# One more whole tile before the Winograd chains, fillers moved between cycles, token sums spread

## The chip, the cores and the metric

The kernel runs on one core of a Trainium2 chip. The metric is the device time of one execution in microseconds. The engines named here are PE (matrix multiply), DVE (vector engine), ACT (scalar engine), POOL (which here only issues transfers) and SP (which issues transfers too). Each works through its own instructions strictly in the order in which they were emitted, and waits where an operand, or a buffer that it writes, is not ready.

## The reference

A decoder trunk of two layers on one sequence of 512 tokens of width 1024, float32. Layer 0 mixes tokens by attention over three groups of heads with different dilations, layer 1 by a gated linear recurrence. After each mixer stands a gated feed-forward block, and each of these four parts is wrapped in RMS norms with a residual:

```python
def conv_ffn(x, w_up, conv_w, conv_b, w_down):
    u = causal_dwconv(x @ w_up, conv_w, conv_b)          # width 6144, 3 taps along the tokens
    g, v = u[..., :D_FF], u[..., D_FF:]
    return (jax.nn.gelu(g, approximate=True) * v) @ w_down

# per layer: x = x + rms_norm(mixer(rms_norm(x)));  x = x + rms_norm(conv_ffn(rms_norm(x)))
```

The change concerns the two feed-forward blocks: their up projection (1024 to 2 times 3072 features) and its beginning.

## The kernel before, in words

**Arithmetic.** Every float32 operand of a product is split into two rounded halves, high and low: ACT copies the operand into the high half (`split`, L211), DVE subtracts it from the operand to get the low half (L212). A product then takes three matmuls: high times high, high times low, low times high.

**The up projection.** The 3072 hidden features are worked through in 12 groups `j` of 256, each with a gate half and a value half of 256 columns. A 128-column piece of it for all 512 tokens is called a tile; `b` 0 and 1 are the two gate tiles of a group, 2 and 3 its two value tiles. After the matmuls of a tile, `begin` (L880 on) starts the convolution: ACT writes the own tap and bias into `u` (L859), DVE adds the two other taps (L863, two instructions of 128x511 and 128x510), and then ACT applies gelu to a gate tile (L881), or DVE multiplies a value tile into its gate tile (L885).

Groups 0 and 1 are computed directly; a tile is 48 matmuls of 256 columns. Groups 2 to 11 (`SEVEN`) are computed with a Winograd form of Strassen's scheme: a 256-column half of a group is one "chain", which needs seven products of half the tokens by half the features instead of eight. There are 20 chains in a block. A chain's products are its steps, numbered 1, 5, 2, 6, 3, 7, 4 in their order of time; each is 12 matmuls of 256 columns. Steps 5, 6, 7, 4 multiply sums and differences of token blocks (`T`, called token sums), which `token_sums` makes on DVE (L1025, L1022) and splits once per block from copies `B` of the normed input. Steps of one chain share two PSUM banks: ACT copies the result of steps 1, 5 and 6 out to `part` (L1159) before a later step adds to the same place; DVE adds these back (L1163 after step 3, L1168 after step 7).

**Weights of a chain.** A `raw` buffer receives the four blocks of a chain's weights (SP, L408). Four sums of blocks are made in place, three by accumulating transfers that POOL issues (L248; `ahead`, `left`, `across`, each sent off once the split of the old value is done), one by DVE (L274). Seven splits give the seven left operands; they are written `w11`, `s1`, `w12`, `s2`, `s3`, `s4`, `a22`. At most 14 halves are alive at a time, and three raw buffers.

**Order of the work around the change.** In `seven` (L1177) all steps stand in numbered places: chain n has the cycle of ten places from 10n, with its steps at the places of `AT` (1: 0, 5: 1, 2: 2, 6: 4, 3: 5, 7: 8, 4: 13, so that step 4 falls into the next cycle). `free_slots` (L253) names the places in between that take fillers. The fillers are, first, the quarters of the two value tiles of group 1 (12 matmuls each, four to a tile, L1127 to L1129), and then the first products of the down projection (`rows`, two to each of 20 hidden tiles k), each of which needs a split of a row of down weights and a split of a finished hidden tile. A filler and a step take PE equally long. `slot` emits one place's matmuls, then what had been put off to it, then a tick. At each tick `pump` emits the next one or two splits, in an order that `stream` sets by due places, and steps that run beside (norms, token sums) go on by one after as many ticks as they last yielded.

**Before the chains**, the norm's last token tiles are transposed on PE and split (`transposed`, L570): ACT high half from PSUM, DVE low half from PSUM, and ACT's plain copy `B` from PSUM for the token sums (L588). Then come the gate and value tiles of group 0, in halves of the tokens; the two gate tiles of group 1, whole; and the chains.

Of the kernel before, what the change touches and what calls it, by code (L numbers as in the profile page):

```python
# [11 lines left out]
F32 = mybir.dt.float32  # L12
F32R = mybir.dt.float32r
I32 = mybir.dt.int32
AF = mybir.ActivationFunctionType
ALU = mybir.AluOpType
# [22 lines left out]
SEVEN = range(2, 12)  # L39
TAIL, REST = 16, range(20, 24)  # L40
AT = {1: 0, 5: 1, 2: 2, 6: 4, 3: 5, 7: 8, 4: 13}
CYCLE = 10
# [83 lines left out]
def kernel(  # L126
# [25 lines left out]
    nc = tc.nc  # L152
# [100 lines left out]
    def free_slots(n):  # L253

        end = CYCLE * n
        free = [CYCLE * c + r for c in range(n) for r in ((6, 7, 9) if c < 2 or c > 13 else (6, 7))][2:] + [end, end + 1]
        assert not {CYCLE * c + a for c in range(n) for a in AT.values()} & set(free)
        return free

    def stream(i0, n):  # L260

        items = []
        for c in range(n):
            i, o = i0 + c, CYCLE * c

            def left(i=i):
                add_block(i, "w11", 2)

            def across(i=i):
                add_block(i, "s1", 0)  # L270

            def lower(i=i):
                x = blocks(i)
                nc.vector.tensor_tensor(x["w12"], x["w12"], x["s1"], op=ALU.add)  # L274

            if c:
                items.append((o - 11, (None, lambda i=i: ahead(i))))
            for at, item in (
                (-6, ("w11", "w11")), (-5.9, (None, left)), (-4.4, ("s1", "s1")), (-4.3, (None, across)),
                (0.4, ("w12", "w12")), (5, ("s2", "s1")), (5.1, (None, lower)), (7, ("s3", "w11")),  # L280
                (8.5, ("s4", "w12")), (10.6, ("a22", "a22")),
            ):
                if isinstance(item[0], str):
                    item = ((i, item[0]), lambda i=i, h=item[1]: [blocks(i)[h]], item[0] == "a22")
                items.append((o + at, item))
        free = free_slots(n)
        direct = up["direct"]
        at = 8
        for key, loads, cuts, length in direct:
            u = free[at]  # L290
            if loads:
                items.append((u - EARLY, (None, loads)))
            items.append((u - 1, ((i0, key), cuts, False)))
            at += length
        return [item for _, item in sorted(items, key=lambda x: x[0])]
# [117 lines left out]
    def chunk():  # L413
        i = state["next"]
        state["next"] += 1
        return i
# [16 lines left out]
    def later(n, f):  # L433
        due.append([n, f])
# [109 lines left out]
    copies = {}  # L544
# [25 lines left out]
                nc.scalar.activation(o.rearrange("p (k b j) -> p k b j", k=4, j=32), src, AF.Copy)  # L570

    def transposed(t, xs, hT, keep):
        banks = []
        for i in range(2):
            ps = psum("tr")
            for k in range(4):
                nc.tensor.transpose(ps[:, k * P : (k + 1) * P], xs[i][:, k * P : (k + 1) * P], ident)
            ps3 = ps.rearrange("p (k c) -> p k c", k=4)
            hi = hT[0][:, 4 * i : 4 * i + 4, t * P : (t + 1) * P]
            lo = hT[1][:, 4 * i : 4 * i + 4, t * P : (t + 1) * P]  # L580
            nc.scalar.activation(hi, ps3, AF.Copy)
            nc.vector.tensor_tensor(lo, ps3, hi.bitcast(F32), op=ALU.subtract)
            banks.append(ps)
        if keep:
            copies[t] = []
            for ps in banks:
                o = gen(s="B")
                nc.scalar.activation(o, ps, AF.Copy)  # L588
                copies[t].append(o)

    def first_transposed(t, i, ks=range(4)):

# [112 lines left out]
    def feat_tile(i, m, hT, sink):  # L705
        ps = psum()
        W = take(i, m)
        for n in (0, 256):
            feat(W, hT, ps, n, n + 256)
        done()  # L710
        rest = sink(ps)
        tick()
        if rest:
            rest()
# [135 lines left out]
    def ffn(layer, hT, post, pre):  # L850
# [20 lines left out]
        def begin(b, ps, j, minus=False, apart=False):  # L871
            m = b % 2
            k = 2 * j + m
            u, taps = conv(ps, 24 * (b // 2) + k, minus)
            if apart:
                later(0, taps)
            else:
                taps()
            if b < 2:
                gv[k] = u  # L880
                return lambda: nc.scalar.activation(u, u, AF.Gelu_apprx_tanh)  # L881
            g = gv[k]

            def gate():
                nc.vector.tensor_tensor(g, g, u, op=ALU.mult)  # L885
                ready.add(k)

            return gate

        def tiles(j, i, bs):  # L890
            for b in bs:
                feat_tile(i, b % 2, hT, lambda ps: begin(b, ps, j))

        def gen_load(*srcs):
            o = []
# [13 lines left out]
        for k in range(REST[0]):  # L909
            w = ffn_w_down[layer][k * P : (k + 1) * P, 0:512].rearrange("(k p) c -> p k c", p=P)  # L910
            o, load = gen_load(w)
# [3 lines left out]
        T = []  # L915
        side(token_sums(T), 3)
        for j in range(SEVEN[0] - 1):
# [3 lines left out]
            else:  # L921
                feat_tiles(2, hT, lambda b, ps: begin(b, ps, j)(), True)
        tiles(SEVEN[0] - 1, chunk(), (0, 1))
        prep, run = down(act, post, pre)
        return run(seven(hT, T, begin, chunk(), lambda: prep(2)))

    def down(act, post, pre):

# [139 lines left out]
    def token_sums(T):  # L1068

        assert len(sides) == 1, len(sides)  # L1070
        d = dp.tile([P, 4, D], F32, name=nm("x_kept"))
        nc.gpsimd.dma_start(d, X[0])
        kept.append(d)
        wide = token_homes(False)
        T.extend([[h[:, 2 * k : 2 * k + 2] for k in range(2)] for h in wide[n : n + 2]] for n in range(0, 8, 2))
        b11, b12, b21, b22 = ([copies[t + a][i] for a in range(2)] for i, t in ((0, 0), (0, 2), (1, 0), (1, 2)))

        def part(n, a, b):
            hi, lo = (h[:, :, P * a : P * a + P] for h in wide[2 * n : 2 * n + 2])
            split(hi, lo, b[a].rearrange("p (k t) -> p k t", k=4))  # L1080

        for a in range(2):
            difference(b11[a], b11[a], b12[a])
        yield 1
        for a in range(2):
            part(0, a, b11)
        yield 1
        for a in range(2):
            difference(b12[a], b22[a], b12[a])
            negative(b22[a], b11[a], b22[a])  # L1090
        yield 1
        for a in range(2):
            part(1, a, b22)
        yield 1
        for a in range(2):
            part(2, a, b12)
        yield 1
        for a in range(2):
            negative(b21[a], b22[a], b21[a])
        yield 1  # L1100
        for a in range(2):
            part(3, a, b21)
# [71 lines left out]
    def seven(hT, T, begin, last, prep):  # L1174
# [4 lines left out]
        def finish(b, ps, j, minus=False):  # L1179
            later(2, begin(b, ps, j, minus, True))  # L1180
# [13 lines left out]
            if pair[-1] == 3:  # L1194
                done(2)

        fill = []
        for m in range(2):
            fill += quarters(last, m, hT, lambda ps, m=m: finish(2 + m, ps, SEVEN[0] - 1))
        fill += [lambda k=k, p=p: rows(k, p) for k in range(REST[0]) for p in ((0, 1), (2, 3))]  # L1200
        steps = {}
        n = 0
# [5 lines left out]
        free = free_slots(n)  # L1208
# [631 lines left out]
```

## Time and profile before

| what | us |
|---|---|
| median of 3 runs (lowest, highest) | 1414.52 (1412.24, 1415.29) |
| the profiled execution, its own time | 1413.27 |
| span of that execution in the trace | 1411.5 |
| PE busy within the span | 1384.2 |
| DVE busy within the span | 1105.5 |
| ACT busy within the span | 816.4 |
| first chain of layer 0 starts at | 522.13 |

A row of the timeline shows its start and its busy time, and how many equal instructions it holds; a bracket at its end is the idle time of that engine just before it and what ended it. Ends of matmuls are modelled and overlap the next start, so the pace of PE is read from starts. The windows view gives, for a stretch, the busy time of each engine and then the TensorE clock that was granted, the DMA share and GB/s. The two feed-forward blocks lie at about 480 to 860 us and 1020 to 1411 us, and behave alike.

### The profile page before, as it was taken

How to read it: one execution, taken by the hardware profiler on the slowest of the kernel's cores; microseconds unless marked ns; L12 is line 12 of the kernel's file. 1: busy time of each engine (PE TensorE's matmuls, PEld its weight loads, DVE VectorE, ACT ScalarE, POOL GpSimd, SP SyncE). 2: the span in 40 equal slices, each digit the busy share in tenths (PEclk: the TensorE clock that was granted, in tenths of full speed). 3: DMA queues.
4: the chain of work that ended last, by engine and by line, in shares of the span. 5: the costliest groups of instructions: out<-in, count | busy, mean ns of one | idle time of the engine just before them, and what ended most of it. 6: DMA issues, size and time to landing. Idle time of an engine off the chain costs nothing.

```text
span 1411.5 us, 25678 instructions
## 1 busy us (share of the span) xinstructions
PE 1384.2 (98%) x9749; PEld 1285.7 (91%) x9749; DVE 1105.5 (78%) x2173; ACT 816.4 (58%) x1686; POOL 236.7 (17%) x392
## 2 busy tenths in 40 slices
PE   9999999999999989999999999999998999999998
PEld 7989999999998889999999888989898999999886
DVE  6576898888866898888887758669788988888753
ACT  7343565453636576666666545489566666666641
POOL 0341342231310112122110001000102221211000
PEclk9999999999999999999999999999999999999999
DMA  7543354655565458676764532332446776765411
GB/s 224 183 139 120 121 182 138 188 153 172 168 195 197 144 150 186 166 177 164 176 169 126 177 127 92 120 118 68 160 139 146 176 178 172 173 165 149 164 61 59
DMA packets 70643, 214.62 MB, mean 152 GB/s; under 512 B 10816, under 2 KB 14360, under 8 KB 58744
## 3 DMA queue, kind: packets, MB, share of 16 engines
q1 hardware_dynamic: 42552, 153.34, 32.0%
q0 software_dynamic: 27120, 58.60, 20.3%
q8 instruction: 76, 1.25, 0.4%
q10 hardware_dynamic: 848, 1.05, 0.2%
q14 instruction: 47, 0.39, 0.1%
HBM read 193.99 MB, written 18.96 MB: 151 GB/s over the span
## 4 chain that ended last, share of the span: by engine, by line
PE 74%; issue 12%; DVE 10%; ACT 2%; DMA 1%; POOL 0%; DVEq 0%; SPq 0%; ACTq 0%; POOLq 0%
PE ps L1150 35%; PE acc L477 19%; PE v L1347 7%; PE ps L477 6%; DVE wlo L212 3%; PE v L1285 1%; DVE u L863 1%; PE O L1559 1%; PE S L1493 1%; DMA raw<-in_attn_w_qkv_dram 1%; PE ps L1127 1%; PE ps L1128 1%; PE ps L1129 1%; PE S L1441 1%; DVE x_sb L662 1%
## 5 line engine op out<-in xcount | busy, mean ns | idle before, releaser
L212 DVE TENSOR_TENSOR wlo<-raw,whi 128x512 fp32r<-128x512 f32 x628 | 417.3, 685 | 117.5 <-ACT whi L211 113.7
L211 ACT ACTIVATE whi<-raw 128x512 fp32r<-128x512 f32 x628 | 375.8, 626 | 165.9 <-PE ps L1150 55.9
L1150 PE MATMUL ps<-T,whi 128*128 128x256 f32 x1344 | 241.5, 279 | 11.8 <-ACT part L1159 11.8
L477 PE MATMUL ps<-hT,whi 128*128 128x256 f32 x1376 | 239.6, 278 | 1.3 <-ACT whi L211 1.3
L1150 PE MATMUL ps<-hT,whi 128*128 128x256 f32 x1344 | 239.5, 278 | 0.0
L1150 PEld LDWEIGHTS ps<-T,whi 128*128 128x128 f32 x1344 | 208.1, 190 | 15.4 <-ACT part L1159 12.2
L477 PEld LDWEIGHTS ps<-hT,whi 128*128 128x128 f32 x1376 | 209.9, 189 | 2.2 <-ACT whi L211 1.5
L1150 PEld LDWEIGHTS ps<-hT,whi 128*128 128x128 f32 x1344 | 205.8, 189 | 1.4
L477 PE MATMUL ps<-hT,wlo 128*128 128x256 f32 x688 | 191.0, 278 | 0.4 <-DVE wlo L212 0.4
L1150 PE MATMUL ps<-T,wlo 128*128 128x256 f32 x672 | 186.9, 278 | 0.0
L1150 PE MATMUL ps<-hT,wlo 128*128 128x256 f32 x672 | 186.2, 277 | 0.0
L248 POOL DMA_DIRECT2D raw<-in_ffn_w_up_dram x120 | 104.1, 930 | 416.9 <-DVE wlo L212 380.8
L477 PE MATMUL acc<-whi,ahi 128*128 128x512 f32 x336 | 131.4, 391 | 0.0
L477 PE MATMUL acc<-whi,alo 128*128 128x512 f32 x336 | 131.0, 390 | 0.1
L477 PE MATMUL acc<-wlo,ahi 128*128 128x512 f32 x336 | 130.8, 389 | 0.0
L477 PEld LDWEIGHTS ps<-hT,wlo 128*128 128x128 f32 x688 | 130.1, 189 | 0.6 <-DVE wlo L212 0.6
L1150 PEld LDWEIGHTS ps<-T,wlo 128*128 128x128 f32 x672 | 127.4, 190 | 0.0
L1150 PEld LDWEIGHTS ps<-hT,wlo 128*128 128x128 f32 x672 | 127.2, 189 | 0.0
L1159 ACT ACTIVATE part<-ps 128x256 f32<-128x256 f32 x168 | 63.7, 379 | 86.7 <-PE ps L1150 83.9
L1347 PE MATMUL v<-whi,hT 128*128 128x512 f32 x320 | 107.0, 397 | 0.0
L863 DVE SCALAR_TENSOR_TENSOR u<-ps,cols,u 128x511 f32<-128x511 f32 x112 | 83.6, 746 | 2.0
L1150 PE MATMUL ps<-last,whi 128*128 128x256 f32 x448 | 80.1, 278 | 2.3 <-DVE ps L1168 2.2
(224 smaller groups left out, 2481.8 us busy)
## 6 DMA issues: line engine op xcount, KB each, us to landing
raw<-in_ffn_w_up_dram SPq DMA_DIRECT2D x48, 1024.0 KB
raw<-in_attn_w_qkv_dram SPq DMA_DIRECT2D x34, 1024.0 KB
raw<-in_ffn_w_up_dram POOLq DMA_DIRECT2D x120, 256.0 KB, 5.4
raw<-in_ffn_w_down_dram SPq DMA_DIRECT2D x14, 1024.0 KB
dw<-in_ffn_w_down_dram SPq DMA_DIRECT2D x40, 256.0 KB
raw<-in_lru_w_in_dram SPq DMA_DIRECT2D x8, 1024.0 KB
turned<-T POOLq DMA_DIRECT2D x26, 256.0 KB, 2.6
ft<-turned POOLq DMA_DIRECT2D x104, 64.0 KB, 4.7
```

Source lines behind the costliest of these rows:

```text
L211: nc.scalar.activation(hi, raw, AF.Copy)
L212: nc.vector.tensor_tensor(lo, raw, hi.bitcast(F32), op=ALU.subtract)
L248: nc.gpsimd.dma_start(blocks(i)[to], plan[i][3][0][0][:, 4 * b : 4 * b + 4, :], accum_op=ALU.add)
L477: mm(dst, l[a], r[b], start=start and n == 0, stop=stop and n == 2)
L662: nc.vector.scalar_tensor_tensor(xc, u[i], y, xc, op0=ALU.mult, op1=ALU.add)
L863: nc.vector.scalar_tensor_tensor(u[:, d:], ps[:, : S - d], wc, u[:, d:], op0=ALU.mult, op1=ALU.add)
L1127: mm(ps[0][:, c], W[0][k // 4][:, k % 4, :], hT[0][:, k, c], start=n == k == 0, stop=False, skip_group_check=True)
L1128: mm(ps[0][:, c], W[0][k // 4][:, k % 4, :], hT[1][:, k, c], start=False, stop=False, skip_group_check=True)
L1129: mm(ps[0][:, c], W[1][k // 4][:, k % 4, :], hT[0][:, k, c], start=False, stop=k == KD - 1, skip_group_check=True)
L1150: mm(dst, W[wa][0][:, k, :], right[n](ha, k), start=n in (1, 5) and k == q == 0, stop=k == 3 and q == 2, skip_group_check=True,)
L1159: later(1, lambda: nc.scalar.activation(to, dst, AF.Copy))
L1347: mm(bank, hT[a][:, k, t * P : (t + 1) * P], W[b][k % 2][:, 0, :], start=(k, a, b) == (0, 0, 0), stop=(k, a, b) == (KD - 1, 1, 0),)
```

## The change

Four things are changed, in both feed-forward blocks.

- `ffn`: the first value tile of group 1 is computed whole in front of the chains, and only its multiplication into the gate tile is put off by two places (`later(2, ...)`).
- `free_slots` and `seven`: the fillers are the four quarters of the second value tile and the 40 row products. The first cycle takes the four quarters at its places 3, 6, 7, 9; every other cycle takes two fillers. Before, the first cycle had one filler, the second three, cycles 2 to 13 two, cycles 14 to 19 three. The first row product moves from place 46 to place 16.
- `token_sums`: two of its yields become 2, so that two groups of its steps come one tick later.
- `transposed`: where copies are kept (the two feed-forward blocks), ACT first copies the transposed tile from PSUM to `B`, and then both the high half (ACT) and the low half (DVE) are taken from `B` in SBUF.

```diff
-        free = [CYCLE * c + r for c in range(n) for r in ((6, 7, 9) if c < 2 or c > 13 else (6, 7))][2:] + [end, end + 1]
+        free = [3, 6, 7, 9] + [CYCLE * c + r for c in range(1, n) for r in (6, 7)] + [end, end + 1]
...
-        at = 8
+        at = 4
         for key, loads, cuts, length in direct:
...
     def transposed(t, xs, hT, keep):
-        banks = []
+        copies[t] = []
...
-            nc.scalar.activation(hi, ps3, AF.Copy)
-            nc.vector.tensor_tensor(lo, ps3, hi.bitcast(F32), op=ALU.subtract)
-            banks.append(ps)
-        if keep:
-            copies[t] = []
-            for ps in banks:
+            if keep:
                 o = gen(s="B")
                 nc.scalar.activation(o, ps, AF.Copy)
                 copies[t].append(o)
+                ps3 = o.rearrange("p (k c) -> p k c", k=4)
+            nc.scalar.activation(hi, ps3, AF.Copy)
+            nc.vector.tensor_tensor(lo, ps3, hi.bitcast(F32), op=ALU.subtract)
...
-        def tiles(j, i, bs):
+        def tiles(j, i, bs, wait=None):
             for b in bs:
-                feat_tile(i, b % 2, hT, lambda ps: begin(b, ps, j))
+                sink = lambda ps, b=b: begin(b, ps, j)
+                feat_tile(i, b % 2, hT, sink if wait is None else lambda ps: later(wait, sink(ps)))
...
         tiles(SEVEN[0] - 1, chunk(), (0, 1))
+        i = chunk()
+        tiles(SEVEN[0] - 1, i, (2,), 2)
         prep, run = down(act, post, pre)
-        return run(seven(hT, T, begin, chunk(), lambda: prep(2)))
+        return run(seven(hT, T, begin, i, lambda: prep(2)))
...
         for a in range(2):
             part(0, a, b11)
-        yield 1
+        yield 2
...
         for a in range(2):
             part(1, a, b22)
-        yield 1
+        yield 2
...
-        fill = []
-        for m in range(2):
-            fill += quarters(last, m, hT, lambda ps, m=m: finish(2 + m, ps, SEVEN[0] - 1))
+        fill = quarters(last, 1, hT, lambda ps: finish(3, ps, SEVEN[0] - 1))
```

Three places show how the instructions move. First, DVE from the taps of the first gate tile of group 0 (`u_6383`) on. `B` rows are the token differences, `wlo` low halves of weights. Before:

```order
L863 SCALAR_TENSOR_TENSOR u_6383<-ps_6184,cols_1406,u_6383 128x511
L863 SCALAR_TENSOR_TENSOR u_6383<-ps_6184,cols_1406,u_6383 128x510
L1025 TENSOR_TENSOR B_6250<-B_6252,B_6250 128x512
L1022 SCALAR_TENSOR_TENSOR B_6252<-B_6035,B_6252 128x512
L1025 TENSOR_TENSOR B_6292<-B_6294,B_6292 128x512
L1022 SCALAR_TENSOR_TENSOR B_6294<-B_6065,B_6294 128x512
L212 TENSOR_TENSOR wlo_6393<-raw_5919,whi_6392 128x512
L212 TENSOR_TENSOR wlo_6397<-raw_5919,whi_6396 128x512
```

and with the change:

```order
L861 SCALAR_TENSOR_TENSOR u_6383<-ps_6184,cols_1406,u_6383 128x511
L861 SCALAR_TENSOR_TENSOR u_6383<-ps_6184,cols_1406,u_6383 128x510
L212 TENSOR_TENSOR wlo_6389<-raw_5919,whi_6388 128x512
L212 TENSOR_TENSOR wlo_6393<-raw_5919,whi_6392 128x512
L861 SCALAR_TENSOR_TENSOR u_6422<-ps_6185,cols_1406,u_6422 128x511
L861 SCALAR_TENSOR_TENSOR u_6422<-ps_6185,cols_1406,u_6422 128x510
L1026 TENSOR_TENSOR B_6241<-B_6250,B_6241 128x512
L1023 SCALAR_TENSOR_TENSOR B_6250<-B_6035,B_6250 128x512
```

The four differences stood right behind the taps of the first gate tile; now two weight splits and the next tile's taps stand between. Second, ACT up to the first copy to `part` of the first chain. `u_6631` (before) and `u_6627` (now) are the second gate tile of group 1, `u_6692` is the value tile that now stands in front, `last` the last token sum. Before:

```order
L881 ACTIVATE u_6563<-u_6563 128x512
L859 ACTIVATE u_6631<-ps_6582,cols_1410 128x512
L211 ACTIVATE whi_6635<-raw_6320 128x512
L211 ACTIVATE whi_6640<-raw_6017 128x512
L881 ACTIVATE u_6631<-u_6631 128x512
L211 ACTIVATE whi_6660<-raw_6017 128x512
L1159 ACTIVATE part_6658<-ps_6645 128x256
```

and with the change:

```order
L211 ACTIVATE whi_6572<-raw_6017 128x512
L879 ACTIVATE u_6559<-u_6559 128x512
L857 ACTIVATE u_6627<-ps_6578,cols_1410 128x512
L211 ACTIVATE whi_6633<-raw_6320 128x512
L211 ACTIVATE whi_6638<-raw_6017 128x512
L879 ACTIVATE u_6627<-u_6627 128x512
L857 ACTIVATE u_6692<-ps_6643,cols_1410 128x512
L211 ACTIVATE last_6299<-B_6036 128x4x128
L211 ACTIVATE last_6299<-B_6065 128x4x128
L211 ACTIVATE whi_6700<-raw_6017 128x512
L211 ACTIVATE whi_6707<-raw_6320 128x512
L211 ACTIVATE whi_6726<-raw_6017 128x512
```

The copy to `part` (`part_6724`) is the next row. Between the gelu of the second gate tile and that copy stood one instruction; now six stand there. Third, PE at the end of step 2 and after it. Before, step 6 (on `T`) follows step 2 at once:

```order
L1150 MATMUL ps_6665<-hT_5664,whi_6510 128x256 x2
L1150 MATMUL ps_6665<-hT_5664,wlo_6511 128x256
L1150 MATMUL ps_6645<-T_6298,whi_6576 128x256 x2
L1150 MATMUL ps_6645<-T_6298,wlo_6577 128x256
L1150 MATMUL ps_6645<-T_6298,whi_6576 128x256 x2
```

and with the change a quarter (`ps_6769`) follows, 12 matmuls of which three are shown, and then step 6:

```order
L1151 MATMUL ps_6732<-hT_5664,whi_6506 128x256 x2
L1151 MATMUL ps_6732<-hT_5664,wlo_6507 128x256
L1128 MATMUL ps_6769<-hT_5664,whi_6388 128x256
L1129 MATMUL ps_6769<-hT_5664,whi_6388 128x256
L1130 MATMUL ps_6769<-hT_5664,wlo_6389 128x256
```

One filler moved to between steps 2 and 6.

## The prediction

> **What bounds the kernel now.** I read PE's waits first, then its timeline around the longest, then what it waited for, engine by engine. PE is busy for 98% of the span, so only places where it stands still, or runs slow, are to be had. In the view of waits, PE's largest group by far is
>
> ```profile
> PE ps L1150 <- ACT part L1159: 11.8, 2, 5.9
> ```
>
> that is, two waits of 5.9 us, one in each feed-forward block. PE's timeline shows the one in layer 0 (first step, end of step 2, step 6, step 7):
>
> ```profile
> 522.13 0.39 PE L1150 MATMUL ps<-hT,whi 128*128 128x256 f32 x2
> ...
> 526.10 0.28 PE L1150 MATMUL ps<-hT,wlo 128*128 128x256 f32 x1
> 532.26 0.80 PE L1150 MATMUL ps<-T,whi 128*128 128x256 f32 x2 [5.89 <-ACT part L1159]
> ...
> 537.55 0.48 PE L1150 MATMUL ps<-T,whi 128*128 128x256 f32 x2
> ```
>
> and the one in layer 1:
>
> ```profile
> 1072.13 0.79 PE L1150 MATMUL ps<-T,whi 128*128 128x256 f32 x2 [5.94 <-ACT part L1159]
> ...
> 1076.78 0.52 PE L1150 MATMUL ps<-hT,whi 128*128 128x256 f32 x2
> ```
>
> By starts, single matmuls follow each other every 0.11 us, so PE is free at 526.21; the three steps since 522.13 took 1.36 each. It resumes at 532.26: 6.05 lost. Then steps 6 and 3 take 5.29 (532.26 to 537.55) instead of 2.72: another 2.57, because the granted clock has halved (the column behind POOL):
>
> ```profile
> 532.00:534.00 2.00, 1.74 (x8) 1.74 (x9) 1.80 (x3) 2.00 (x5) 1.32 (x2) 0.50 0.35 51
> ```
>
> So 8.62 in layer 0. In layer 1 about 6.1 and, of the 4.65 to 1076.78, half, 2.3: 8.4. Together **17.0 us**.
>
> Why is the copy to `part` late, when step 1, which it reads, ended at 523.5? ACT's timeline:
>
> ```profile
> 526.87 0.76 ACT L859 ACTIVATE u<-ps,cols 128x512 f32<-128x512 f32 x1
> 527.54 1.14 ACT L211 ACTIVATE whi<-raw 128x512 fp32r<-128x512 f32 x2
> 530.79 0.63 ACT L881 ACTIVATE u<-u 128x512 f32<-128x512 f32 x1 [2.12 <-DVE u L863]
> 531.32 0.61 ACT L211 ACTIVATE whi<-raw 128x512 fp32r<-128x512 f32 x1
> 531.84 0.36 ACT L1159 ACTIVATE part<-ps 128x256 f32<-128x256 f32 x1
> ```
>
> The copy stands behind the gelu of group 1's second gate tile, and that waits for its taps on DVE, which start at 529.17 because DVE works off its queue without a hole:
>
> ```profile
> 526.16 1.28 DVE L212 TENSOR_TENSOR last<-B,last 128x512 fp32r<-128x512 f32 x2
> 527.36 1.29 DVE L212 TENSOR_TENSOR wlo<-raw,whi 128x512 fp32r<-128x512 f32 x2
> 528.57 0.69 DVE L274 TENSOR_TENSOR raw<-raw 128x512 f32<-128x512 f32 x1
> 529.17 1.53 DVE L863 SCALAR_TENSOR_TENSOR u<-ps,cols,u 128x511 f32<-128x511 f32 x2
> 530.61 4.23 DVE L212 TENSOR_TENSOR wlo<-raw,whi 128x512 fp32r<-128x512 f32 x6
> ```
>
> So DVE's backlog, through ACT's order, stops PE. Starts also give the paces used below: DVE 0.60 for an instruction of 512 columns, 1.44 for a pair of taps; ACT 0.52 for a split, 0.67 for the copy into `u`, 0.53 for a gelu.
>
> **The change, part by part.**
>
> *The value tile in front.* It is 48 matmuls, four steps' worth: 4 x 1.36 = 5.44 us. It moves, PE does nothing more in sum. The first chain starts at 522.13 + 5.44 = 527.57; steps 1, 5, 2 and then a quarter (third order piece) take 4 x 1.36, so PE comes to step 6 at **533.0**, 6.8 later than now.
>
> *What ACT and DVE do until then.* I walked both queues in their new order, starting from the last transposed tiles:
>
> ```profile
> 495.00 1.07 ACT L581 ACTIVATE hT<-tr 128x512 fp32r<-128x512 f32 x2
> 497.82 1.20 ACT L588 ACTIVATE B<-tr 128x512 f32<-128x512 f32 x2 [1.75 <-DVE hT L582]
> 498.92 1.08 ACT L581 ACTIVATE hT<-tr 128x512 fp32r<-128x512 f32 x2
> ...
> 500.75 1.28 DVE L1025 TENSOR_TENSOR B<-B,B 128x512 f32<-128x512 f32 x2
> ```
>
> ACT's copies wait 1.75 for DVE's reads of the same PSUM tile. With the copy first that wait goes, but the high half now queues behind the copy, so DVE's first differences move only from 500.75 to about 500.35 by the walk: -0.4. Bounds: the whole 1.75 gained; or, if both copies delay the high halves, 1.2 lost. I take -0.4, since the same four ACT instructions per tile bound it.
>
> *The spread yields.* Now:
>
> ```profile
> 506.84 1.52 DVE L863 SCALAR_TENSOR_TENSOR u<-ps,cols,u 128x511 f32<-128x511 f32 x2
> 508.28 0.68 DVE L1025 TENSOR_TENSOR B<-B,B 128x512 f32<-128x512 f32 x1
> ...
> 510.93 1.28 DVE L212 TENSOR_TENSOR wlo<-raw,whi 128x512 fp32r<-128x512 f32 x2
> ...
> 514.95 1.29 DVE L212 TENSOR_TENSOR T<-B,T 128x512 fp32r<-128x512 f32 x2 [1.28 <-ACT T L211]
> ...
> 508.44 1.28 ACT L881 ACT_TABLE_LOAD   x1 [2.15 <-DVE u L863]
> ...
> 510.27 1.14 ACT L211 ACTIVATE whi<-raw 128x512 fp32r<-128x512 f32 x2
> ```
>
> Between 508.28 and 510.93 the four differences fill the time in which ACT loads the gelu table and applies it. They move behind the next tile's taps (first order piece), and the low halves that now come next need high halves that stand behind that gelu: first one done at 510.8. So a **new hole on DVE of about 2.4 us**, while the 1.28 ahead of `T` closes. Further on, two differences and two subtractions of `last` fall behind the taps in question (second piece): 4 x 0.60 = -2.4. These taps, done at 530.61 now, are then done at 530.6 - 0.4 - 2.4 + 2.4 - 1.3 = **528.9**.
>
> *From there to `part`.* ACT has gelu 0.54, the value tile's copy 0.67, two splits of `last` 1.10, three splits 1.56, and the copy 0.36: 4.2, done at 533.2. PE comes at 533.0: it waits about **0.3**. Step 3's low half is then ready at 534.7, where PE comes at 534.7: nothing. Bounds of the wait: none if the hole is smaller; 2.7 if the hole of 1.28 stays and the -0.4 becomes +0.7. I take 0.4.
>
> *A transfer on that path.* Ahead of the gate tile's copy, ACT now splits `s2`, which needs the transfer `across`; POOL sends it off once a split is done. Now:
>
> ```profile
> 521.12 1.73 POOL L248 DMA_DIRECT2D raw<-in_ffn_w_up_dram  x2 [3.10 <-DVE wlo L212]
> ...
> DMA to landing us min/median/max: 5.5/5.5/5.5
> ...
> DMA to landing us min/median/max: 4.1/5.0/7.8
> ```
>
> (the first landing line is of the issues of 521 to 522.5, the second of all 24 between 490 and 600). It would be issued at about 520.7 and land at 524.8 to 526.2, which fits: the gelu behind it starts only about then. The longest seen, 7.8, gives 528.5 and is a rival.
>
> *The second cycle.* Between step 3's low half (534.7) and the addition that chain 1's step 4 waits for, DVE has 28 instructions of 0.60 and four pairs of taps: 22.6, and about 1 of holes, so 558.3. PE gets there after 18 slots, 533.3 + 18 x 1.36 = 557.8. A wait of 0.5. If DVE had no hole: none; with a hole like the 2.4: 1.9.
>
> *The later cycles.* The chain of waits shows a cycle with two fillers and, later, one with three:
>
> ```profile
> 673.34 2.75 PE acc L477 x12
> 676.09 9.56 PE ps L1150 x84
> 685.65 2.75 PE acc L477 x12
> ...
> 724.00 2.75 PE acc L477 x12
> ...
> 737.73 2.75 PE acc L477 x12
> ```
>
> 12.31 and 13.73 us, and PE and DVE in stretches of each kind (PE, PEld, DVE, ACT, POOL):
>
> ```profile
> 600.00:612.00 12.00, 12.00 (x96) 11.55 (x95) 10.29 (x18) 7.84 (x16) 2.74 (x4) 1.00 0.82 192
> 740.00:800.00 60.00, 60.00 (x402) 54.70 (x401) 48.32 (x77) 37.69 (x68) 2.58 (x3) 1.00 0.50 151
> ```
>
> DVE is busy 10.55 of 12.31, or 11.06 of 13.73. The last six cycles lose a filler with its work and look like the first kind: cover of 1.76 per cycle. Rows that move from place 46 to 16 bring their splits (2 x 0.60 per pair) into cycles that lose quarters: nothing in sum. Cost 0; without that cover, rival C.
>
> **Sum.** Gain 17.0; new waits 2 x (0.4 + 0.5) = 1.8; net 15.2, against the profiled execution's own 1413.27 (1.25 below the median of the runs): **1398**.
>
> **Rivals.**
>
> *A, half the gain.* `across` lands after 7.8, or another step on this path is as late. Then split 0.52, gelu 0.53, copy 0.67 and taps 1.44 end at 531.7 instead of 528.9, and PE waits 3.1 at step 6. 2 x 2.7 more: 1403. If the clock halves again, 2 x 2.57 more: 1408. For it: landings of 7.8 exist. Against: this one took 5.5. The nearest rows on the clock, a short idle that left it whole:
>
> ```profile
> 212.00 0.50 PE L1150 MATMUL ps<-last,whi 128*128 128x256 f32 x2 [1.59 <-DVE ps L1168]
> ...
> 210.00:215.00 5.00, 3.41 (x21) 2.75 (x20) 4.43 (x8) 1.76 (x3) 0.00 (x0) 1.00 0.00 0
> ```
>
> so 1.59 costs itself alone and 5.89 halves the clock; 3.1 lies between, hence both times. The Trainium skill ("TensorE: Matmul & The Clock Gate", section "What's actually happening") puts the drop after an idle window of about 3.4 us, free-running, so that its edge moves. Both rows agree with it; by it 3.1 would cost only itself, and A would be 1403.
>
> *B, no gain.* DVE is the bound of the whole stretch, and the wait moves along with the work: the taps end past 534.8, PE waits 6 again, 1413. For it: DVE had no hole from 514.95 on. Against: ahead of step 6, PE gets 6.8 of work and DVE only the low halves that stood there already.
>
> *C, slower.* DVE bounds the twelve late cycles (six per block) that shrink from 13.73 to 12.31. To give back the gain and 0.2% more, 15.2 + 2.8 = 18.0, each needs 1.5 of PE idle, a demand on DVE of 13.8 with its waits. At 14.0 it is 12 x 1.69 = 20.3: 1418. For it: PE has the least cover there. Against: 10.55 in the same kind of cycle, with PE full.
>
> **Chances.** A measurement cannot tell less than 0.2% (2.8 us) from no change. The forecast (waits of at most 2 us per block) 0.72, A 0.15, B 0.07, C 0.06. Its own range is 1395 (no wait left, 1396.3, and the lowest run lies 1.0 below the profiled one) to 1401; the whole range adds A: 1395 to 1408. Faster 0.87 (forecast and A), same 0.07 (B), slower 0.06 (C).
>
> **What would show it.** Right: no wait of PE above 1 us at step 6 of the first chain, granted clock 1.00 from 520 to 545 and 1060 to 1085; the first chain at about 527.6; a DVE hole of some 2.4 behind the first taps; a wait of at most 1 for chain 1's step 4; cycles of 12.31 to the end; ACT's copies to `B` no longer waiting for DVE. Wrong: a PE idle of 3 or more between 526 and 570, or PE losing time between 700 and 800.

## The result, and the profile after

The changed kernel takes 1400.73 us (median of 4 runs, 1398.50 to 1401.71) against 1414.90 of the kernel before; the ratio is 0.9901 (95% interval 0.9883 to 0.9919). Measured a second time, with the experiments, it took 1399.01 us (5 runs, 1398.32 to 1402.70) against 1413.77, ratio 0.9900 (0.9885 to 0.9916). The gain is 14 to 15 us, 1.0% of the time, where 15.2 were forecast.

PE's waits in the changed kernel, the groups that matter here (engine, tile and line; what was waited for; us in total, times, longest):

```profile
PE ps L1151 <- DVE ps L1169: 4.6, 5, 1.6
PE tr L577 <- DVE xs L555: 2.7, 2, 2.0
...
PE ps L1151 <- ACT part L1160: 0.3, 1, 0.3
```

The 11.8 us in two waits for the copy to `part` have shrunk to 0.3. The two stretches that ran at 0.50 before are at full clock; windows of the changed kernel (columns as before, the clock behind POOL):

```profile
520.00:540.00 20.00, 20.00 (x178) 20.00 (x178) 19.83 (x32) 12.97 (x25) 5.17 (x6) 1.00 0.55 101
...
1060.00:1080.00 20.00, 19.67 (x174) 19.48 (x173) 19.12 (x32) 13.83 (x27) 5.16 (x6) 1.00 0.67 143
```

This profile is of the slowest of the first four runs, and something new in it costs 2.8 us. PE's timeline of the changed kernel, at the last transposes of layer 0's norm, and then at the places where chains wait:

```profile
497.85 1.62 PE L577 MATMUL tr<-ident,xs 128*128 128x128 f32 x8 [1.99 <-DVE xs L555]
...
781.75 0.50 PE L1151 MATMUL ps<-last,whi 128*128 128x256 f32 x2 [0.76 <-DVE ps L1169]
...
1093.53 0.51 PE L1151 MATMUL ps<-last,whi 128*128 128x256 f32 x2 [0.87 <-DVE ps L1169]
...
1314.79 0.51 PE L1151 MATMUL ps<-last,whi 128*128 128x256 f32 x2 [0.76 <-DVE ps L1169]
```

and the same transposes in the kernel before:

```profile
496.64 1.10 PE L577 MATMUL tr<-ident,xs 128*128 128x128 f32 x8 [0.83 <-DVE xs L555]
```

PE waits 1.99 instead of 0.83 there, and then the clock is down; windows of the changed kernel:

```profile
495.00:500.00 5.00, 3.01 (x20) 2.81 (x19) 4.52 (x16) 4.82 (x12) 1.47 (x2) 0.83 0.76 315
500.00:505.00 5.00, 5.00 (x39) 5.00 (x39) 4.54 (x8) 4.97 (x10) 0.00 (x0) 0.83 0.63 159
```

What is late ahead of it shows in ACT's timeline of the changed kernel, where ACT waits for a transferred tile of the token mixer:

```profile
479.62 0.64 ACT L565 ACTIVATE hT<-ft 128x512 fp32r<-128x512 f32 x1 [1.51 <-DMA ft<-turned]
```

Before, ACT split that tile from 477.98 on without a wait, and in none of the other 13 profiles does ACT wait more than 0.6 for such a tile. So a transfer of the token mixer landed late here, and PE came to wait 1.2 more; that DVE's norm work handed the delay on to PE is read from the order of the work and not tried. This is 1.2 of waiting and, by estimate, 1.6 of slow clock. Whether it belongs to the change is what one of the runs below asks.

So the span's 11.6 us (1411.5 to 1399.9) are the 17.0 of the old stops, less 2.8 here, less 2.7 of waits of the chains that are new: 0.3 at `part`, 0.76 twice at the end of the last chains, 0.87 in layer 1's second chain. That makes 11.5. (Behind layer 0's block the clock is halved for 3.4 us in both profiles, so that drops out; see the last section.)

### The profile page after: what moved, and what is told of

Same layout as the page of the kernel before. It is cut to its first block, busy times and chain, and to the rows that moved or that the text cites. A ratio compares the mean times of both kernels' runs of the same rounds, so it can differ in the third digit from the quotient of the medians.

```text
span 1399.9 us, 25665 instructions
## 1 busy us (share of the span) xinstructions
PE 1380.9 (99%) x9749; PEld 1282.3 (92%) x9749; DVE 1104.4 (79%) x2173; ACT 814.4 (58%) x1686; POOL 236.3 (17%) x392
## 3 DMA queue, kind: packets, MB, share of 16 engines
q8 instruction: 76, 1.25, 0.4%
## 4 chain that ended last, share of the span: by engine, by line
PE 78%; DVE 9%; ACT 6%; issue 4%; DMA 2%; POOL 0%; DVEq 0%; SPq 0%; ACTq 0%; POOLq 0%
PE ps L1151 36%; PE acc L477 21%; PE ps L477 9%; PE v L1346 7%; DVE wlo L212 2%; PE v L1284 1%; ACT whi L211 1%; DVE xb L1650 1%; PE S L1492 1%; DMA ft<-turned 1%; PE O L1558 1%; DVE u L861 1%; DMA raw<-in_attn_w_qkv_dram 1%; ACT sig L1671 1%; PE S L1440 1%
## 5 line engine op out<-in xcount | busy, mean ns | idle before, releaser
L477 PE MATMUL ps<-hT,whi 128*128 128x256 f32 x1440 | 251.6, 279 | 1.3 <-ACT whi L211 1.3
L1151 PE MATMUL ps<-hT,whi 128*128 128x256 f32 x1344 | 236.9, 276 | 0.0
L477 PEld LDWEIGHTS ps<-hT,whi 128*128 128x128 f32 x1440 | 220.4, 190 | 2.2 <-ACT whi L211 1.5
L1151 PEld LDWEIGHTS ps<-hT,whi 128*128 128x128 f32 x1344 | 203.0, 188 | 0.6
L477 PE MATMUL ps<-hT,wlo 128*128 128x256 f32 x720 | 200.2, 278 | 0.4 <-DVE wlo L212 0.4
L1151 PE MATMUL ps<-hT,wlo 128*128 128x256 f32 x672 | 185.1, 275 | 0.0
L477 PEld LDWEIGHTS ps<-hT,wlo 128*128 128x128 f32 x720 | 136.7, 190 | 0.6 <-DVE wlo L212 0.6
L477 PE MATMUL acc<-whi,ahi 128*128 128x512 f32 x336 | 131.2, 390 | 0.0
L477 PE MATMUL acc<-whi,alo 128*128 128x512 f32 x336 | 131.0, 390 | 0.2
L477 PE MATMUL acc<-wlo,ahi 128*128 128x512 f32 x336 | 130.8, 389 | 0.0
L1151 PEld LDWEIGHTS ps<-hT,wlo 128*128 128x128 f32 x672 | 126.2, 188 | 0.0
```

The source lines that it names most:

```text
L477: mm(dst, l[a], r[b], start=start and n == 0, stop=stop and n == 2)
L1151: mm(dst, W[wa][0][:, k, :], right[n](ha, k), start=n in (1, 5) and k == q == 0, stop=k == 3 and q == 2, skip_group_check=True,)
```

## The experiments

The theory, as it stood in the prediction: DVE's backlog stops PE at step 6 of the first chain, and the change gives PE 6.8 us of other work while DVE works it off; call it "time for PE". Its rival, "shorter queues": the gain comes from the two small edits, the spread token sums and the copies first, which take work out of the way of the copy to `part`. The kernels are told by what they undo.

**The tile and the fillers alone.**

```diff
-        yield 2
+        yield 1
...   (both spread steps; transposed as before: both halves from PSUM, copy last)
```

> The value tile in front and the fillers of the change, with the token sums' steps and the copies as before. Theory 'time for PE': the 6.8 us that PE has more before step 6 are what removes the stop; the taps then end where they ended before (530.6), the copy to part is done at about 533.8 and PE, at 533.0, waits 0.7 per block instead of 0.3: 1400 to 1402 us. Rival 'shorter queues': spread steps and copies are needed; then PE waits 3 or more at step 6 in each block, the clock drops there, and the time is 1406 or more.

1398.65 us, ratio 0.9892 (0.9875 to 0.9909). PE's timeline of this kernel at step 6 of the first chains:

```profile
533.47 0.50 PE L1153 MATMUL ps<-T,whi 128*128 128x256 f32 x2 [0.83 <-ACT part L1162]
...
1066.05 0.50 PE L1153 MATMUL ps<-T,whi 128*128 128x256 f32 x2 [0.82 <-ACT part L1162]
```

0.8 per block where 0.7 was expected, at full clock, and a time even below that of the whole change and below the expected range. "Shorter queues" falls: the small edits are not needed.

**No tile: the small edits alone**, on the kernel before.

```diff
-        yield 1
+        yield 2
...   (both; transposed as changed; ffn, free_slots and seven as before)
```

> The kernel before with the spread token sums and the new copies alone; no tile in front, fillers as before. Theory 'time for PE': the taps come 1.3 to 2 us earlier, but two splits of the last sums now stand behind the gelu (1.1 us), so PE still waits 5 to 5.5 us at step 6 and the clock still drops: 1412.5 to 1415. Rival 'shorter queues': the wait falls under 3 us without a clock drop, 1402 to 1407.

1411.50 us, ratio 0.9980 (0.9970 to 0.9991). PE's timeline of it:

```profile
531.68 0.80 PE L1148 MATMUL ps<-T,whi 128*128 128x256 f32 x2 [5.50 <-ACT part L1157]
...
1068.43 0.79 PE L1148 MATMUL ps<-T,whi 128*128 128x256 f32 x2 [5.47 <-ACT part L1157]
```

The waits came out as the theory had them, 0.4 and 0.5 less than before; the time is 1 us below its range. The interval lies below 1, so the small edits by themselves do gain something, 1.3 to 4.2 us. The two profiles show 0.9 of it as shorter waits. Another 1.6 lies behind layer 0's block, where the clock halves in the profile of before and not in this one (last section); that is no work of the edits. The rest was not traced. It is still far from the 7 to 12 us that "shorter queues" asked for.

**The old copies**, everything else changed.

```diff
-            if keep:
-                o = gen(s="B")
-                nc.scalar.activation(o, ps, AF.Copy)
...
+        if keep:
+            for ps in banks:
+                o = gen(s="B")
+                nc.scalar.activation(o, ps, AF.Copy)
```

> The changed kernel with the copies of the transposed tiles as before (high and low half from PSUM, copy last). Theory 'time for PE': within 1.5 us of the changed kernel (1400.7); if the low halves' new wait for ACT behind each token tile (0.46 us a time in the changed kernel's trace, four times in each block) delays the norm, this one is up to 2 us faster. Rival 'shorter queues': the old wait of 1.75 us on ACT comes back and shows as a wait of PE at step 6, 3 us slower.

1399.84 us, ratio 0.9906 (0.9892 to 0.9921): within 1.5 of the change. PE waits 0.74 and 0.75 at step 6, against 0.32 twice with the new copies (the second profile of the change, below). The new copies are worth 0.4 per block, and the norm is not delayed by them: from the first product of layer 1's mixer to that layer's last transposes it takes 157.2 us in both.

**The old yields**, everything else changed.

```diff
-        yield 2
+        yield 1
...   (both)
```

> The changed kernel with the token sums' steps one tick apart as before. The hole of 2.56 us on DVE behind the first taps should be filled again, the second gate tile's taps have two differences and two subtractions (2.4 us) more ahead of them. Theory 'time for PE': the two cancel to 1.3 us, PE waits at most 1.5 us at step 6 of a block, the time is within 2 us of 1400.7. Rival 'shorter queues': 4 us or more slower.

1397.30 us, ratio 0.9883 (0.9868 to 0.9897), the lowest of the kernels so far. At step 6 PE waits 0.41 and 0.36. The hole on DVE is gone, as one sees in DVE's timeline of this kernel, where the four differences stand behind the first taps again:

```profile
507.17 1.52 DVE L861 SCALAR_TENSOR_TENSOR u<-ps,cols,u 128x511 f32<-128x511 f32 x2
508.62 0.68 DVE L1026 TENSOR_TENSOR B<-B,B 128x512 f32<-128x512 f32 x1
...
511.27 1.28 DVE L212 TENSOR_TENSOR wlo<-raw,whi 128x512 fp32r<-128x512 f32 x2
```

and with it the second chain's wait of 0.87 is gone. What the spread took from the queue ahead of the gelu it gave back in the hole, as the prediction's sum said; what the sum priced too low is that DVE stays behind until the second chain.

**The change once more**, unaltered, for the 2.8 us of layer 0's norm.

> The changed kernel once more, unaltered. In its first profile PE waited 1.99 us for the last normed tile of layer 0 and ran at half clock until 501.6, some 2.8 us lost. Theory 'only that execution' (the attention's transfer that the norm stage waits for landed late): this profile shows the 0.7 to 0.8 us of the other kernels there and full clock, and the median falls to 1398 to 1400. Rival 'the copies': the wait of about 2 us and the half clock come again, 1400 to 1401.5.

1399.01 us. PE's timeline of the second profile: the transposes, the first chain, step 6, and step 4 of the second chain, in layer 0; then steps 6 and 4 in layer 1.

```profile
497.25 1.09 PE L577 MATMUL tr<-ident,xs 128*128 128x128 f32 x8 [0.80 <-DVE xs L555]
...
528.14 0.39 PE L1151 MATMUL ps<-hT,whi 128*128 128x256 f32 x2
...
534.07 0.50 PE L1151 MATMUL ps<-T,whi 128*128 128x256 f32 x2 [0.32 <-ACT part L1160]
...
559.79 0.50 PE L1151 MATMUL ps<-last,whi 128*128 128x256 f32 x2 [0.87 <-DVE ps L1169]
...
1065.62 0.50 PE L1151 MATMUL ps<-T,whi 128*128 128x256 f32 x2 [0.32 <-ACT part L1160]
...
1091.34 0.50 PE L1151 MATMUL ps<-last,whi 128*128 128x256 f32 x2 [0.86 <-DVE ps L1169]
```

The wait of 1.99 and the half clock behind it are not there, nor in any other profile. They belong to that one execution. In this profile the chains wait 3.9 us: 0.32, 0.87 and 0.76 in layer 0 and nearly the same in layer 1.

**One quarter less before step 6.**

```diff
-        free = [3, 6, 7, 9] + [CYCLE * c + r for c in range(1, n) for r in (6, 7)] + [end, end + 1]
+        free = [6, 7, 9] + [CYCLE * c + r for c in range(1, n) for r in ((6, 7, 9) if c < 2 else (6, 7))] + [end, end + 1]
```

> The changed kernel with no quarter between steps 2 and 6 of the first chain; that filler goes to the second cycle, which has three. PE then comes to step 6 1.36 us earlier. Theory 'time for PE': it waits 0.3 + 1.36 = 1.7 us there in each block (1.0 to 1.7 in layer 0), without a clock drop, and gains up to 0.9 per block where chain 1's step 4 waited: 0 to 3 us slower than the changed kernel. Rival 'the quarter is not needed': no wait at step 6 beyond 0.5, 1 to 2 us faster.

1400.38 us, ratio 0.9905 (0.9890 to 0.9920). PE's timeline:

```profile
535.38 0.50 PE L1151 MATMUL ps<-T,whi 128*128 128x256 f32 x2 [1.65 <-ACT part L1160]
...
1068.66 0.51 PE L1151 MATMUL ps<-T,whi 128*128 128x256 f32 x2 [1.64 <-ACT part L1160]
```

1.7 were expected: 1.36 us of PE work less is 1.33 us of wait more, and the second chain's waits went, as they should with three fillers there. The time is 1.4 above that of the change measured beside it, within the 0 to 3 expected.

**One quarter before step 6, in the kernel before.**

```diff
-        free = [CYCLE * c + r for c in range(n) for r in ((6, 7, 9) if c < 2 or c > 13 else (6, 7))][2:] + [end, end + 1]
+        free = [3] + [CYCLE * c + r for c in range(n) for r in ((6, 7, 9) if c < 2 or c > 13 else (6, 7))][3:] + [end, end + 1]
```

> The kernel before with one edit: the first cycle's one quarter stands between steps 2 and 6, not behind step 3. PE has 1.36 us more ahead of step 6 and nothing else moves there. Theory 'time for PE' (each us of PE's work ahead takes a us off the stop): the wait falls from 5.9 to about 4.5 in each block, the clock still drops: 1411 to 1413. Rival: the wait moves along with the work and stays at 5.5 or more, 1414 to 1415.

1414.67 us, ratio 1.0009 (0.9998 to 1.0020): no gain, where 2 to 3 us were expected. PE's timeline of it tells why:

```profile
533.06 0.72 PE L1150 MATMUL ps<-T,whi 128*128 128x256 f32 x2 [4.54 <-ACT part L1159]
...
543.91 0.51 PE L1150 MATMUL ps<-last,whi 128*128 128x256 f32 x2 [0.65 <-DVE ps L1168]
...
571.30 0.39 PE L1150 MATMUL ps<-last,whi 128*128 128x256 f32 x1 [1.23 <-DVE ps L1168]
...
1071.65 0.80 PE L1150 MATMUL ps<-T,whi 128*128 128x256 f32 x2 [4.54 <-ACT part L1159]
...
1078.05 0.50 PE L1150 MATMUL ps<-T,whi 128*128 128x256 f32 x2 [1.40 <-ACT part L1159]
...
1110.48 0.39 PE L1150 MATMUL ps<-last,whi 128*128 128x256 f32 x1 [0.85 <-DVE ps L1168]
```

The quarter had stood at place 9, behind step 7 (not behind step 3, as the expectation puts it). The wait at step 6 fell by 1.35 and 1.40, just as the theory says, and the quarter was then missing further on: PE waits 0.65 at step 4 of the same chain in layer 0 and 1.40 at step 7 in layer 1, and at the third chain's step 4 another 1.23 and 0.85, all of them new. In sum the two blocks wait 13.2 us and not 11.8. The clock still drops. A filler that only changes its place in the cycle moves the wait; it doesn't give DVE time. The theory was right about step 6 and left out what comes behind it; the rival had the time right, but the wait at step 6 did not stay.

**The tile in front, but the fillers of the first two cycles as before.**

```diff
-        free = [3, 6, 7, 9] + [CYCLE * c + r for c in range(1, n) for r in (6, 7)] + [end, end + 1]
+        free = [9, 16, 17, 19] + [CYCLE * c + r for c in range(2, n) for r in ((6, 7, 9) if c > 17 else (6, 7))] + [end, end + 1]
```

> The changed kernel's tile in front, with the fillers of the first two cycles as before (one in the first, behind step 3; three in the second). PE has 5.44 us more ahead of step 6 and not 6.8, and 4.1 less in the rest of the first cycle. Theory 'the tile alone is enough': a wait of 1.7 at step 6 and nothing else, at full clock: 1400 to 1402. Rival 'DVE is behind through the whole first cycle': waits of 2 to 3 more per block at steps 3, 7 or 4 of the first chain, 1404 or more.

1403.72 us, ratio 0.9935 (0.9920 to 0.9950). PE's timeline, and DVE (third) beside PE (first) in a window:

```profile
534.74 0.50 PE L1151 MATMUL ps<-T,whi 128*128 128x256 f32 x2 [1.66 <-ACT part L1160]
...
539.18 0.50 PE L1151 MATMUL ps<-T,whi 128*128 128x256 f32 x2 [1.40 <-ACT part L1160]
...
1067.73 0.51 PE L1151 MATMUL ps<-T,whi 128*128 128x256 f32 x2 [1.67 <-ACT part L1160]
...
1072.64 0.51 PE L1151 MATMUL ps<-T,whi 128*128 128x256 f32 x2 [1.87 <-ACT part L1160]
```

```profile
530.00:540.00 10.00, 6.95 (x59) 6.56 (x58) 9.96 (x17) 7.29 (x15) 2.59 (x3) 1.00 0.61 118
```

Here too the first cycle's one filler is at place 9, behind step 7; and the last two cycles have three fillers, so that the waits of 0.76 at the end are not there. The 1.7 at step 6 came as expected; at step 7 there are 1.4 and 1.9 more, between the two theories. DVE is busy for 9.96 of the 10 us. So the tile alone brings some 9 us (1413.08, measured beside it, to 1403.72), and the four fillers in the first cycle the other 5. In the profiles (the two blocks, timed as under "A faster version") the difference to the change is 3.0, with the 1.5 at the end saved here, so some 4.5. The time that DVE needs is spread over the whole first cycle, not over the stretch up to step 6.

**One filler in the sixth to eleventh cycle, three in the last six**, for rival C.

```diff
-        free = [3, 6, 7, 9] + [CYCLE * c + r for c in range(1, n) for r in (6, 7)] + [end, end + 1]
+        free = [3, 6, 7, 9] + [CYCLE * c + r for c in range(1, n) for r in ((6,) if 5 <= c <= 10 else (6, 7, 9) if c > 13 else (6, 7))] + [end, end + 1]
```

> The changed kernel with one filler, not two, in the sixth to eleventh cycle and three in each of the last six, as before. Tests rival C (DVE sets the pace of the later cycles). Theory 'cover enough': cycles with one filler take 10.9 us of PE, DVE needs some 10 of them; no wait of PE above 0.3 between 600 and 700, and the wait of 0.76 at the last chain's end is gone: 1398. Rival 'DVE at its bound': waits of 0.5 or more in these cycles, six in each block, 1405 or more.

1399.24 us (1397.01 to 1402.69), ratio 0.9901 (0.9883 to 0.9918). The chain of waits of this kernel in the cycles with one filler, and a window:

```profile
632.94 1.39 PE acc L477 x6
634.33 9.56 PE ps L1151 x84
643.88 1.39 PE acc L477 x6
```

```profile
640.00:700.00 60.00, 60.00 (x481) 57.99 (x480) 52.63 (x85) 40.84 (x77) 13.05 (x15) 1.00 0.73 179
```

Cycles of 10.94 us, PE full, DVE with 12% to spare. Rival C is out: even 1.4 us less than in the change leaves DVE time. With three fillers in the last cycle, PE's waits of 0.76 at the end of the last chains are gone.

**Three fillers behind the last chain**, on the kernel with the old yields.

```diff
-        free = [3, 6, 7, 9] + [CYCLE * c + r for c in range(1, n) for r in (6, 7)] + [end, end + 1]
+        free = [3, 6, 7, 9] + [CYCLE * c + r for c in range(1, n) for r in ((6,) if c == 10 else (6, 7))] + [end, end + 1, end + 2]
```

> The kernel with the token sums' steps one tick apart (the fastest so far, 1397.3) with one row filler moved from the eleventh cycle to behind the last chain, so that three and not two stand ahead of the last chain's step 4. Theory: the wait of 0.76 there in each block goes (1.4 us more time for DVE), and the eleventh cycle, 10.9 us of PE with one filler, is still not bound by DVE: 1395.8, 1.5 faster. Rival 'the cycle is at DVE's bound' (rival C of the prediction): PE loses 0.5 us or more per block in the eleventh cycle, no gain.

1396.96 us, ratio 0.9883 (0.9868 to 0.9898). Both waits of 0.76 are gone and the eleventh cycle has none, so the trace agrees with the theory. The median moved by 0.3 and not 1.5, and the profile of this kernel is one with a half clock behind layer 0's feed-forward block, where that of the old yields is not (last section); at this size the medians don't decide. Within the two blocks alone, as measured under "A faster version" below, the profile is 1.6 shorter than that of the old yields.

**And of the two spread steps only the second.**

```diff
         for a in range(2):
             part(1, a, b22)
-        yield 1
+        yield 2
```

> The kernel with one filler moved behind the last chain, and of the two spread steps only the second (the one behind the second token sum). The four differences then fill DVE's time behind the first taps as before (no hole of 2.56), and two subtractions of the last sums (1.2 us) fall behind the second gate tile's taps. Theory: the wait of 0.41 at step 6 goes, no wait comes at the second chain's step 4: 0.4 less per block than with one filler moved alone (1397.0), 1396 to 1396.5. Rival: the subtractions that fell back delay step 3 or 7 by as much, no gain.

1397.49 us, ratio 0.9883 (0.9867 to 0.9898). The wait at step 6 is gone; but 0.34 and 0.39 came at step 4 of the second chain, where the theory had none. So nothing is gained that can be seen, as the rival said, though the new wait is not at step 3 or 7, where it had put it.

**Of the two spread steps only the first.**

```diff
         for a in range(2):
             part(1, a, b22)
-        yield 2
+        yield 1
```

> The changed kernel with only the first of the two spread steps (the one behind the first token sum); the second is back. Theory 'the first one makes the hole': DVE idles 2.5 us behind the first taps as in the changed kernel, PE waits about 0.5 at step 6 and about 0.9 at the second chain's step 4 in each block: the changed kernel's time, 1399 to 1400.5. Rival 'the second one does': no hole and none of the waits of 0.9, 1397.5.

1401.05 us, ratio 0.9909 (0.9895 to 0.9924). DVE's timeline behind the first taps:

```profile
508.17 1.52 DVE L861 SCALAR_TENSOR_TENSOR u<-ps,cols,u 128x511 f32<-128x511 f32 x2
512.25 1.29 DVE L212 TENSOR_TENSOR wlo<-raw,whi 128x512 fp32r<-128x512 f32 x2 [2.56 <-ACT whi L211]
```

The hole is the first yield's. PE waits 0.47 and 0.48 at step 6 and 0.87 and 0.85 at the second chain's step 4, as the theory said; the time is 0.5 above its range.

**A faster version.** The change without its spread steps is 2 us below the change (1397.30, and 1396.96 with the third filler at the end, against 1399.01 and 1400.73). The medians of the three kernels around 1397 can't be told from one another. The profiles tell more when only the two blocks are timed, from the norm's last transposes (the row of L577) to the first product behind the block in layer 0 (L477) and to the last matmul in layer 1: together 748.6 us before, 735.6 in the change's second profile, 733.6 with the old yields, 732.0 with the third filler too. PE's waits in the chains fall along with it, 3.9, 2.3 and 0.8 in the last three.

## Why the prediction was right, step by step

**The bound and the sum.** Right: a chain from DVE's backlog through ACT's order to PE, 17.0 us, and the change removes it. 1398 was forecast and 1400.73 measured, 1399.01 the second time; the net gain was 15.2 by the sum and 14.2 and 14.8 by the medians. That these lie so close is in part luck. The two blocks by themselves became 13.0 us shorter (748.6 to 735.6, second profile), so the sum promised some 2 too much; the clock behind layer 0's block, halved in the profile of before and not in this one, adds 1.6 to the difference of these two profiles. That ACT's order hands DVE's delay on to PE is read from the timelines; no run moved the copy ahead of the gelu.

**The tile in front.** The first chain was to start 30.9 us behind the norm's last transposes (527.57 less 496.64). In the second profile it is 528.14 less 497.25, also 30.9.

**The copies.** From the transposes to DVE's first differences it took 4.11 us (496.64 to 500.75); with the change 3.76 (497.25 to 501.01). -0.4 was taken, and the old copies put 0.4 back at step 6. ACT's copies to `B` no longer wait for DVE.

**The hole.** 2.4 us forecast, 2.56 seen in both layers, and the one of 1.28 closed.

**Taps and `part`.** ACT's timeline of the second profile around the copy:

```profile
525.52 0.64 ACT L211 ACTIVATE whi<-raw 128x512 fp32r<-128x512 f32 x1 [4.41 <-DMA raw<-in_ffn_w_up_dram]
...
529.85 0.64 ACT L879 ACTIVATE u<-u 128x512 f32<-128x512 f32 x1 [1.45 <-DVE u L861]
530.39 0.76 ACT L857 ACTIVATE u<-ps,cols 128x512 f32<-128x512 f32 x1
531.05 1.14 ACT L211 ACTIVATE last<-B 128x512 fp32r<-128x512 f32 x2
532.09 1.66 ACT L211 ACTIVATE whi<-raw 128x512 fp32r<-128x512 f32 x3
533.66 0.36 ACT L1160 ACTIVATE part<-ps 128x256 f32<-128x256 f32 x1
```

The gelu starts at 529.85 where the walk had 528.9; 0.6 of that is the later norm. From the gelu to the end of the copy 4.2 were forecast and are seen (529.85 to 534.02). PE waits 0.32; 0.4 was taken. The transfer `across` lands at 525.5, in the 524.8 to 526.2 of the forecast, and rival A did not come. ACT did stand idle 4.41 us for it, but its copy into `u` behind that (526.58 to 527.34) was still done 0.9 before DVE came to the taps at 528.23: that much later it could have landed at no cost.

**The second chain.** 0.5 taken, 0.87 and 0.86 measured, within the bounds of 0 and 1.9.

**The later cycles: the step that failed.** "Cost 0" held for their pace, 12.31 each. As a whole the term was wrong: it overlooked the end of the last chain, whose step 4 needs DVE's addition as every chain's does, with two fillers ahead of it and not three. It costs 0.76 in each block. By the letter, "PE losing time between 700 and 800", which was to show the prediction wrong, came true with this wait at 781; what it stood for, a loss in each of the late cycles, did not. With the 0.4 too little for the second chain in each block, the new waits are 3.9 and not 1.8. With them the net gain is 13.1, as the blocks show it, and the sum gives 1400.2.

**The rivals.** B and C are out: the taps did not move back, and cycles of 10.9 still run at PE's pace. What B described exists on a smaller scale: in the kernel before with an early quarter 1.4 us of waiting moved along with the work. Rival A left it open whether 3.1 us of idle would halve the clock; the last section shows that 1.66 can be enough.

**What was not seen ahead** is that the change without its spread steps is faster. The prediction had both halves of it, the hole and the queue ahead of the gelu, and their sum of nothing at step 6, but it didn't ask what the hole does to DVE past that step.

## What to carry to other kernels

Where PE stops because an elementwise engine is behind, look for how long that engine stays behind, not only for the place where PE meets it: moving one filler there moved the wait, and 5.4 us in front with four fillers behind removed it. An engine with a backlog should not be given work whose operand stands behind a wait of another engine; the instructions that filled DVE's time during ACT's table load were worth more there than out of the way. And when the fillers of a loop are dealt out anew, look at its last round, which has no next one to hide its tail.

## What the runs showed of the hardware

Behind the feed-forward block of layer 0, at the first product of layer 1's mixer, every one of the 14 profiles has the same idle of PE: 1.25 or 1.26 us, then 0.41 more. In 8 of them the clock stays at 1.00, in 6 it halves 1 to 2 us later, for 3.4 us (a mean clock of 0.81 over the 9 us from there). From that product to the first gate product of the mixer it takes 54.7 to 54.8 us in these six and 53.1 in the other eight, so the half clock costs 1.6. The changed kernel, PE's timeline and a window:

```profile
872.28 0.50 PE L477 MATMUL ps<-hT,whi 128*128 128x256 f32 x2 [1.25 <-ACT whi L211]
...
874.00:876.00 2.00, 2.00 (x12) 2.00 (x11) 2.00 (x4) 0.82 (x2) 0.00 (x0) 0.50 0.53 123
```

and the kernel with the old yields:

```profile
870.75 0.50 PE L477 MATMUL ps<-hT,whi 128*128 128x256 f32 x2 [1.25 <-ACT whi L211]
...
872.00:874.00 2.00, 2.00 (x20) 2.00 (x19) 2.00 (x5) 1.29 (x3) 0.00 (x0) 1.00 0.40 74
```

Same kernel code there, same idle, another clock. The 1.99 us in the first profile of the change did it too. At 212 us, in layer 0's mixer, it is the same: 1.59 in the kernel before left the clock whole, and so did 2.64 with the old yields, but 1.80 (only the first spread step) and 1.98 (no early quarter) halved it, for 3.4 us each. So in this kernel an idle of 1.3 to 2.6 us is a draw, worth 1.6 us if it is lost. Runs of one kernel spread over 1 to 6 us; that such draws make the spread is likely and not shown, since only one run of each measurement has a profile.

What decides the draw can be read from where the slow stretches end. Each us at half clock takes 0.25 off the mean of a window of 2 us, so a mean of 0.57 stands for 4 x 0.43 = 1.72 us at half clock. Windows of the kernel before, at the ends of its three slow stretches:

```profile
536.00:538.00 2.00, 2.00 (x13) 2.00 (x12) 1.51 (x3) 0.41 (x1) 0.00 (x1) 0.57 1.03 166
...
882.00:884.00 2.00, 2.00 (x17) 2.00 (x17) 0.00 (x0) 0.00 (x0) 0.00 (x0) 0.88 0.97 378
...
1076.00:1078.00 2.00, 2.00 (x15) 2.00 (x15) 1.74 (x3) 0.23 (x1) 0.00 (x0) 0.74 1.02 163
```

They end at 537.72, 882.48 and 1077.04, which is 101 and 57 steps of 3.413 us apart; the other profiles with several slow stretches, taken the same way, give the same step to within 0.05 us. Up to the last matmul the stretches last one such step (3.4) or two (6.8, at all but one of the waits of 4.5 to 5.9). So in these profiles the clock changes only at the marks of a grid that runs on through the kernel. When the grid of each profile is drawn on to the place behind layer 0's block, the whole idle of 1.66 (1.25 and 0.41) lies between two marks in the six profiles that halve, and a mark cuts it in the eight that don't, so that at most 1.45 lie between two. (In five of the eight the grid is known from the slow stretch behind the last matmul alone.) The length of an idle alone doesn't decide, then, but where it falls on the grid. The border is not sharp: in the kernel with the tile in front and the fillers as before, 1.66 between two marks at step 6 left the clock whole. No run shifted the idle on purpose.

The Trainium skill ("TensorE: Matmul & The Clock Gate", section "What's actually happening") tells of an activity window of about 3.4 us that runs free; the draw and the 3.4 us at half clock agree with a free-running window, but idles well short of 3.4 us were enough here.
